# Listing experts a step behind and interleaving gate products twice a block, in a one-core decoder layer

## Chip, cores, metric

One core of a Trainium2 chip runs the whole layer in one launch. The metric is the device time in microseconds of that core. "Before" was run three times, and a further execution was profiled.

## The reference, cut to what matters

The layer has a combined projection, two groups of attention heads, an output projection, and then PEER: a retrieval of single-neuron experts by product keys. The change concerns PEER alone. T = 256 tokens, D = 2048, 16384 experts numbered 128 * ia + ib, 8 heads with 16 experts each per token:

```python
va, ia = lax.top_k(sa, PEER_TOPK)
vb, ib = lax.top_k(sb, PEER_TOPK)
...
top, sel = lax.top_k(cand, PEER_TOPK)
eidx = jnp.take_along_axis(cidx, sel, axis=-1)
gates = jax.nn.softmax(top, axis=-1)
...
act = jax.nn.gelu(jnp.einsum('thed,td->the', u[eb], xb))
w = gb * act
out = jnp.einsum('the,thed->td', w, v[eb])
```

Then come layer norms and a gated per-layer embedding.

## The kernel before, in words

PEER is done in two ways at once. The first 88 tokens are *sparse*: their rows of u and v are gathered by indirect DMA (`gb`, four buffers, 88 gathers of u and 88 of v, 1.05 MB each) and multiplied and summed on VectorE (L867, L877). The other 168 tokens (NDT) are *dense*: all of u is read and multiplied on TensorE, one block of 128 experts for each ia (L214, `ps_u`, 16 matmuls of 128x168), and GELU of it goes to a table A with a row for each expert. The rows ia 0 to 67 are part 0 (A0 and A1), ia 68 to 127 part 1 (A2). A 32-bit matmul is two instructions in the trace, so that a block of 16 matmuls is 32 of them.

`gate_work` multiplies the table by the gates. For three tokens at a time (56 groups for the 168 tokens) VectorE makes one-hot matrices of ib (`ohb`) and ia (`eq`), ScalarE scales `eq` by the two halves of the gates (`hi`, `lo`), TensorE multiplies them (`ps_G`, two matmuls per token) and counts the experts used (`ps_cnt`, one matmul per token, added up in a PSUM bank of its own over all tokens), and VectorE multiplies A by the product (L983). Each `yield` ends a step; whoever drives it decides how many steps come after a block.

`list_work` then writes A to DRAM (`s_w`), ranks the experts that any token uses, and makes lists of them: for each ia of the part, VectorE makes a one-hot row (`row`, L1069) and two columns (`blk`, L1070 and L1072), and TensorE adds their product to `ps_list` (L1074). Six such items are a step (`LISTED`). From the lists come `idxV` and `idxW`.

Part 0's gate work and list run beside the blocks ia 68 to 127 of u. Then v is done for listed experts alone, in blocks of 128: `v_fetch` gathers 128 rows of v (`vf`, five buffers shared with u's weights) and their weights (`wc`) by two indirect DMAs on GpSimd's queue, and `v_mm` adds 16 matmuls to six PSUM banks (L1199). There are 46 blocks of part 0 and 40 of part 1, fetched up to four ahead. Part 1's gate work and list run beside the first 46 blocks, four steps after each of the first 27 blocks and one after each later one; what is left is run after block 42. After block 46 a branch on a register, loaded from `total`, skips 42 spare blocks that are needed only if the lists overflow. Each engine has a branch.

`gathers(n)` paces the sparse gathers: it adds n to a sum and starts a gather for each whole one. They share GpSimd's queue with the fetches of v. The paces are GU, GUG and GUL beside blocks of u, and GVG and GV beside blocks of v. A gather waits for the buffer of the fourth before it, and the row in that buffer is used on VectorE in the order written out in the program.

`keep` holds the kept instructions of each engine in the order of the program; the matmuls of blocks and of gate products are not kept, and a scheduler places them.

Of the kernel before, what the change touches and what calls it, by code (L numbers as in the profile page):

```python
# [19 lines left out]
P = 128  # L20
# [36 lines left out]


GQ = 1.8
GU, GUG, GUL = 0.80, 0.80, 0.5  # L60
GV, GVG = 0.7, 0.65
GSCALE = 2.0 ** 15
GB = 3

LISTED = 6

EARLY, HEARLY = 5, 7
OHB = 4
# [94 lines left out]
def build(tc, a, out):  # L163
# [7 lines left out]
    def pbank(pool, name, tag="bank", bufs=4):  # L171
        return pool.tile([P, 512], F32, name=name, tag=tag, bufs=bufs)
# [765 lines left out]
            dst, dst, ALPHA, ps.rearrange("p (j t) -> p j t", j=ND)[:, :, :n],  # L938
            op0=ALU.mult, op1=ALU.add))

    def gate_work(oh, parts, s0, ns, group):


        cnt = pbank(pa, "ps_cnt")

        def one_hot(t0, n):
            def rows(x, m):
                return x[:, None, :].to_broadcast([P, n, m])

            def cols(x, m):  # L950
                return x[:, t0:t0 + n, None].to_broadcast([P, n, m])

            ohb = oh.tile([P, group, P], F16, name="ohb", tag="ohb", bufs=OHB)
            eq = oh.tile([P, group, ns], F16, name="eq", tag="eq", bufs=OHB)
            hi = oh.tile([P, group, ns], F16, name="hi", tag="hi", bufs=OHB)
            lo = oh.tile([P, group, ns], F16, name="lo", tag="lo", bufs=OHB)
            keep(nc.vector.tensor_tensor(eq[:, :n], rows(io128[:, s0:s0 + ns], ns), cols(iaT, ns),  # L957
                                         op=ALU.is_equal))
            keep(nc.vector.tensor_tensor(ohb[:, :n], rows(io128, P), cols(ibT, P),
                                         op=ALU.is_equal))  # L960
            for j in range(n):
                t = slice(t0 + j, t0 + j + 1)
                nc.scalar.mul(hi[:, j, :], eq[:, j, :], ghf[:, t])  # L963
                nc.scalar.mul(lo[:, j, :], eq[:, j, :], glf[:, t])  # L964
            return ohb, eq, hi, lo

        def product(t0, n, ohb, eq, hi, lo):
            ps = pbank(pa, "ps_G")
            for j in range(n):
                o = ps[:, j * ns:(j + 1) * ns]  # L970
                nc.tensor.matmul(o, ohb[:, j, :], hi[:, j, :], start=True, stop=False)
                nc.tensor.matmul(o, ohb[:, j, :], lo[:, j, :], start=False, stop=True)  # L972
                nc.tensor.matmul(cnt[:, :ns], ohb[:, j, :], eq[:, j, :], start=t0 + j == NSP,
                                 stop=t0 + j == T - 1)
            return ps

        def scale(t0, n, ps):
            g = ps[:, :n * ns].rearrange("p (t a) -> p a t", t=n)
            c0 = 0
            for At in parts:  # L980
                dst = At[:, :, t0 - NSP:t0 - NSP + n]
                c1 = c0 + At.shape[1]
                keep(nc.vector.scalar_tensor_tensor(dst, g[:, c0:c1], 1.0 / GSCALE, dst,  # L983
                                                    op0=ALU.mult, op1=ALU.mult))
                c0 = c1

        made, multiplied = [], None
        for t0 in list(range(NSP, T, group)) + [None] * OHB:
            if t0 is not None:
                n = min(group, T - t0)  # L990
                made.append((t0, n, one_hot(t0, n)))
            if multiplied:
                scale(*multiplied)
                multiplied = None
            yield
            if made and (len(made) > OHB - 2 or t0 is None):
                m = made.pop(0)
                multiplied = (m[0], m[1], product(m[0], m[1], *m[2]))
                yield
        if multiplied:  # L1000
            scale(*multiplied)
        yield from list_work(oh, parts, s0, ns, cnt)

    idxV, idxW, over = [], [], []

    def list_work(oh, parts, s0, ns, cnt):


        part = len(idxV)
# [7 lines left out]
        def store(n):  # L1017
            for cut in cuts[:n]:
                load(*cut)
            del cuts[:n]  # L1020

        store(2)
        m = oh.tile([P, ns], F16, name="m", tag="m")
        keep(nc.vector.tensor_scalar(m, cnt[:, :ns], 1.0, None, op0=ALU.min))
        yield
        store(1)

# [23 lines left out]
        keep(nc.vector.tensor_scalar(ov, used[:, ns:ns + 1], -float(CAPS[part] * P), 0.0,  # L1051
                                     op0=ALU.add, op1=ALU.max))
        over.append(ov)
        yield
        store(1)
        pi = oh.tile([P, SEG1], U32, name="pi", tag="pi")[:, :ns]
# [6 lines left out]
        yield  # L1063

        ps = pbank(pa, "ps_list")
        for ia in range(ns):
            row = oh.tile([P, P], F16, name="row", tag="row", bufs=2)
            blk = oh.tile([P, 2, SEG1], F16, name="blk", tag="blk", bufs=2)
            keep(nc.vector.tensor_scalar(row, io128, rank[:, ia:ia + 1], None, op0=ALU.is_equal))  # L1069
            keep(nc.vector.tensor_scalar(blk[:, 0, :ns], io128[:, :ns], pos[:, ia:ia + 1],  # L1070
                                         lin[:, 0:1], op0=ALU.is_equal, op1=ALU.mult))
            keep(nc.vector.tensor_scalar(blk[:, 1, :ns], io128[:, :ns], pos[:, ia:ia + 1],  # L1072
                                         float(ia), op0=ALU.is_equal, op1=ALU.mult))
            keep(nc.tensor.matmul(  # L1074
                ps[:, :2 * SEG1].rearrange("p (i b) -> p i b", i=2)[:, :, :ns],
                row, blk[:, :, :ns], start=ia == 0, stop=ia == ns - 1))
            if ia % LISTED == LISTED - 1:
                store(1)
                yield
        ib = oh.tile([P, SEG1 + 1], F32, name="ib", tag="used")[:, :ns]  # L1080
        iv = gin.tile([P, ns], U32, name=f"idxV{part}")
        iw = gin.tile([P, ns], U32, name=f"idxW{part}")
# [8 lines left out]
    def run(work, n):  # L1091

        for _ in range(n):
            if next(work, "end") == "end":
                return True
        return False
# [74 lines left out]
        return vf, wc  # L1171

    fetched = []
    work = gate_work(ohp, (A0, A1), *PARTS[0], GB)
    for ia in range(SEG1, NIA):
        u_block(ia, W_of(ia))

        made = ia - SEG1
        if made < 38:
            run(work, 3)  # L1180
        elif ia < NIA - 5:
            run(work, 1)
        elif ia == NIA - 5:
            while not run(work, 1):
                pass
            pools.close("a1p", "a0p")
            wcp = pools.open("wcp", "right", bufs=1)
            work = gate_work(ohp, (A2,), *PARTS[1], GB)
            run(work, 1)
        elif ia == NIA - 2:  # L1190
            run(work, 1)
        if ia >= NIA - 4:
            fetched.append(v_fetch(*order.pop(0), sup, wcp, ("wf", "wc")))
        gathers(GUG if made < 38 else GUL)
# [3 lines left out]
    def v_mm(d, vf, wc, last):  # L1198
        return nc.tensor.matmul(psv[d // 3][:, d % 3 * NDT:(d % 3 + 1) * NDT],  # L1199
                                vf[:, d * P:(d + 1) * P], wc, start=False,  # L1200
                                stop=last and (d % 3 == 2 or d == ND - 1))

    def v_bank(pool, n):

        ps = pbank(pool, "ps_v")
        keep(nc.tensor.matmul(ps[:, :n * NDT], ident, zero.to_broadcast([P, n * NDT]),
                              start=True, stop=False))
        return ps

# [5 lines left out]
            dst, dst, ALPHA, psv[b][:, :n * NDT].rearrange("p (j t) -> p j t", j=n),  # L1215
            op0=ALU.mult, op1=ALU.add))

    def v_blocks(n, wpool):

        for _ in range(n):  # L1220
            while order and len(fetched) <= LEAD and (not order[0][0] or len(idxV) > 1):
                fetched.append(v_fetch(*order.pop(0), sup, wpool, ("wf", "wc")))
            block = fetched.pop(0)
            for d in range(ND):
                v_mm(d, *block, False)

    marked = False
    psv = [v_bank(pp, 3) for _ in range(4)] + [v_bank(pa, n) for n in (3, 1)]
    done = False
    for b in range(CAPS[0]):  # L1230
        if b == CAPS[0] - LEAD:
            while not done:
                done = run(work, 1)
        v_blocks(1, wcp)
        if not done:
            done = run(work, 4 if b < 27 else 1)
        gathers(GVG if b < 27 else GV)

    fbp = pools.open("fbp", "right", bufs=1)
    total = fbp.tile([P, 1], mybir.dt.int32, name="total")  # L1240
    keep(nc.vector.tensor_tensor(total, over[0], over[1], op=ALU.add))
    more = nc.values_load(total[0:1, 0:1], min_val=0, max_val=NIA * NKEY)
    with tc.If(more > 0):
# [451 lines left out]
```

## Time and profile before

| what | us |
|---|---|
| median of 3 runs | 1829.73 |
| range of the runs | 1827.35 to 1837.43 |
| profiled execution | 1828.99 |
| its span | 1827.2 |
| busy in the span: TensorE matmuls | 1729.7 |
| VectorE | 1097.7 |
| ScalarE | 554.1 |
| GpSimd | 618.8 |

Times inside the profile count from the start of the span. PE is TensorE (PEld its weight loads), DVE VectorE, ACT ScalarE, POOL GpSimd and SP the engine that issues plain DMAs. A row of waits names the engine and its line, what it waited for, the sum, the number and the longest wait. A row of a stage gives for each engine the busy time and the instructions, then the granted TensorE clock, the DMA engines' busy share and the rate. A timeline row gives start, length, engine, line, operation and count.

### The profile page before, as it was taken

To read this page: it belongs to the slowest core of one execution; us is meant where nothing else is said; L and a number is where in the kernel's file an instruction comes from. 1 tells how busy PE (TensorE), PEld (TensorE's weight loads), DVE (VectorE), ACT (ScalarE), POOL (GpSimd) and SP (SyncE) were. 2 spreads that over 40 slices of the span, in tenths; PEclk is the share of its full clock that TensorE was granted. 3 is DMA by queue.
4 is the path that set the end of the run, shared out by engine and by line. 5 is a ranking of instruction groups with operands and counts; after the bars stand their busy time and mean duration, and the time that the engine had idled before them with its cause. 6 is when DMAs were issued, how large, how long until landed. Compare 5 with 4: busy or idle time off the path is not lost. (4 is left out here: it accounts for less than half of the span.)

```text
span 1827.2 us, 29235 instructions
## 1 busy us (share of the span) xinstructions
PE 1729.7 (95%) x11288; PEld 1594.0 (87%) x11288; DVE 1097.7 (60%) x2243; ACT 554.1 (30%) x1392; POOL 618.8 (34%) x627
## 2 busy tenths in 40 slices
PE   9999999999999999999999999799886949999998
PEld 7888888878899999999999998699886938999887
DVE  5555688654797797444577734635544372352686
ACT  5686477632111000100355410134340000000462
POOL 0233133005445227222233310344446425876000
PEclk9999999999999999999999999799898969999899
DMA  8555644756998999999999997486778929999561
GB/s 295 185 166 166 228 139 162 251 203 234 421 383 351 420 417 417 421 421 420 409 388 385 378 405 296 162 343 245 266 288 311 417 93 356 415 415 397 174 251 67
DMA packets 97105, 555.49 MB, mean 304 GB/s; under 512 B 13364, under 2 KB 16612, under 8 KB 41508
## 3 DMA queue, kind: packets, MB, share of 16 engines
q0 software_dynamic: 43152, 285.45, 39.5%
q1 hardware_dynamic: 52084, 264.99, 38.4%
q10 hardware_dynamic: 1728, 3.15, 0.5%
q8 instruction: 91, 1.49, 0.3%
q14 instruction: 50, 0.41, 0.1%
HBM read 536.67 MB, written 17.04 MB: 303 GB/s over the span
## 5 line engine op out<-in xcount | busy, mean ns | idle before, releaser
L214 PE MATMUL ps_u<-XF,wf 128*128 128x168 f32 x3936 | 594.4, 311 | 10.6 <-DMA wf<-peer_u 10.2
L214 PEld LDWEIGHTS ps_u<-XF,wf 128*128 128x128 f32 x3936 | 569.6, 192 | 21.3 <-issue 15.5
L1199 PE MATMUL ps_v<-wc,vf 128*128 128x168 f32 x2752 | 430.8, 317 | 40.1 <-DMA vf<-v_rows,idxV 24.8
L1199 PEld LDWEIGHTS ps_v<-wc,vf 128*128 128x128 f32 x2752 | 412.5, 197 | 43.9 <-issue 42.7
L124 DVE TENSOR_TENSOR wl<-wf,wh 128x1024 fp32r<-128x1024 f32 (+1 forms) x199 | 212.6, 1091 | 112.4 <-ACT wh L123 111.1
L867 DVE SCALAR_TENSOR_TENSOR gb<-gb,xq 128x2048 f32<-128x2048 f32 x88 | 202.4, 2305 | 103.6 <-DMA gb<-u_rows,eig 103.6
L123 ACT CAST wh<-wf 128x1024 fp32r<-128x1024 f32 (+1 forms) x199 | 172.1, 892 | 223.5 <-DMA wf<-ple_gate 110.6
L877 DVE SCALAR_TENSOR_TENSOR y<-gb,ew,y 128x2048 f32<-128x2048 f32 x78 | 183.0, 2346 | 84.5 <-DMA gb<-v_rows,eig 81.4
L899 POOL DMA_INDIRECT gb<-v_rows,eig x88 | 110.9, 1260 | 251.6 <-DVE eq L957 121.5
L1102 ACT ACTIVATE A<-ps_u 128x168 f32<-128x168 f32 x128 | 39.6, 310 | 488.5 <-PE ps_u L214 476.8
L202 PE MATMUL ps_qk<-X,wh 128*128 128x512 f32 x512 | 185.2, 401 | 0.0
L899 POOL DMA_INDIRECT gb<-u_rows,eig x88 | 95.1, 1081 | 258.0 <-DVE gb L867 148.3
L963 ACT ACTIVATE hi<-eq,ghf 128x68 f16<-128x68 f16 (+1 forms) x336 | 112.7, 335 | 132.3 <-DVE eq L957 110.9
L983 DVE SCALAR_TENSOR_TENSOR A<-ps_G,A 128x18 f32<-128x18 f32 (+2 forms) x168 | 46.8, 307 | 164.7 <-PE ps_G L972 133.1
L204 PE MATMUL ps_qk<-X,wl 128*128 128x256 f32 x512 | 145.7, 285 | 0.0
L1168 POOL DMA_INDIRECT vf<-v_rows,idxV x86 | 111.0, 1291 | 49.3 <-issue 20.0
L1168 POOL DMA_INDIRECT wc<-s_w,idxW x86 | 95.9, 1116 | 83.0 <-DVE ib L1086 34.2
L202 PEld LDWEIGHTS ps_qk<-X,wh 128*128 128x128 f32 x512 | 96.4, 188 | 21.9 <-issue 1.0
L214 PE MATMUL ps_q<-XF,wf 128*128 128x256 f32 x512 | 113.5, 379 | 0.0
L964 ACT ACTIVATE lo<-eq,glf 128x68 f16<-128x68 f16 (+1 forms) x336 | 112.1, 334 | 0.0
L214 PEld LDWEIGHTS ps_q<-XF,wf 128*128 128x128 f32 x512 | 95.8, 190 | 12.4
L204 PEld LDWEIGHTS ps_qk<-X,wl 128*128 128x128 f32 x512 | 96.3, 188 | 2.5 <-issue 1.3
(311 smaller groups left out, 2134.6 us busy)
## 6 DMA issues: line engine op xcount, KB each, us to landing
wf<-peer_u SPq DMA_DIRECT2D x123, 1024.0 KB
wf<-w_qk SPq DMA_DIRECT2D x64, 512.0 KB
wf<-w_out SPq DMA_DIRECT2D x32, 512.0 KB
wf<-peer_wq SPq DMA_DIRECT2D x16, 1024.0 KB
wf<-ple_gate SPq DMA_DIRECT2D x16, 1024.0 KB
s_w<-A SPq DMA_DIRECT2D x14, 672.0 KB
wf<-w_v SPq DMA_DIRECT2D x16, 512.0 KB
wf<-w_sv SPq DMA_DIRECT2D x15, 512.0 KB
```

The lines of the kernel that those rows point to most:

```text
L123: self.order(nc.scalar.copy(wh, src))
L124: self.order(nc.vector.tensor_tensor(wl, src, wh.bitcast(F32), op=ALU.subtract))
L202: nc.tensor.matmul(ps, wh[:, j * P:(j + 1) * P], xt[:, dt, :], start=dt == 0, stop=False)
L204: nc.tensor.matmul(ps[:, :T], wl[:, j * P:(j + 1) * P], xt[:, dt, :T], start=False, stop=dt == ND - 1)
L214: nc.tensor.matmul(ps[:, :T - t0], wf[:, dt * P:(dt + 1) * P], xt[:, dt, t0:], start=dt == 0, stop=dt == ND - 1)
L867: keep(nc.vector.scalar_tensor_tensor(g, g, 1.0, xq[i], op0=ALU.mult, op1=ALU.mult, accum_out=eact[i][:, j:j + 1]))
L877: keep(nc.vector.scalar_tensor_tensor(ys[i], g, ew[i][:, j:j + 1], ys[i], op0=ALU.mult, op1=ALU.add))
L899: keep(nc.gpsimd.indirect_dma_start(out=g, out_offset=None, in_=a[kind], in_offset=bass.IndirectOffsetOnAxis(ap=eig[i][:, 0, j:j + 1], axi ...
L963: nc.scalar.mul(hi[:, j, :], eq[:, j, :], ghf[:, t])
L964: nc.scalar.mul(lo[:, j, :], eq[:, j, :], glf[:, t])
L1168: keep(nc.gpsimd.indirect_dma_start(out=dst, out_offset=None, in_=src, in_offset=bass.IndirectOffsetOnAxis(ap=idx[:, b:b + 1], axis=0)))
L1199: return nc.tensor.matmul(psv[d // 3][:, d % 3 * NDT:(d % 3 + 1) * NDT], vf[:, d * P:(d + 1) * P], wc, start=False, stop=last and (d % 3 = ...
```

## The change

- The list's products are issued one step behind the items that they multiply. `row` and `blk` are taken from the buffers of the one-hot matrices, which gives twelve of each. In part 0 a step has six items as before, in part 1 three.
- Part 1's counts are no longer added up in a bank of their own. Each group's counts stand in the group's bank behind its products, and VectorE takes the first group's counts and then the maximum with each later one (`total_cnt`).
- Beside blocks of v, the steps run twice in a block, after its 8th and its 16th matmul: two steps each time until part 1's experts have been counted, then one.
- `total` is added up as soon as part 1 is counted, and its register is loaded four blocks ahead of the branch. The branch has `preferred_fallthrough_block=False`.
- Part 1's gate work starts with the first block of v: the two single steps run beside the last blocks of u are gone.
- The paces of the gathers are changed.

```diff
-GU, GUG, GUL = 0.80, 0.80, 0.5
-GV, GVG = 0.7, 0.65
+GU, GUG, GUL = 0.77, 0.80, 0.5
+GV, GVG = 0.63, 0.76
...
-LISTED = 6
...
     def product(t0, n, ohb, eq, hi, lo):
...
-                nc.tensor.matmul(cnt[:, :ns], ohb[:, j, :], eq[:, j, :], start=t0 + j == NSP,
-                                 stop=t0 + j == T - 1)
+                if counts is not None:
+                    nc.tensor.matmul(counts, ohb[:, j, :], eq[:, j, :], start=t0 + j == NSP,
+                                     stop=t0 + j == T - 1)
+            if counts is None:
+                for j in range(n):
+                    nc.tensor.matmul(ps[:, n * ns:(n + 1) * ns], ohb[:, j, :], eq[:, j, :],
+                                     start=j == 0, stop=j == n - 1)
             return ps
...
     def scale(t0, n, ps):
...
+            if counts is None:
+                new = ps[:, n * ns:(n + 1) * ns]
+                if t0 == NSP:
+                    keep(nc.vector.tensor_copy(total_cnt, new))
+                else:
+                    keep(nc.vector.tensor_tensor(total_cnt, total_cnt, new, op=ALU.max))
...
+        if part:
+            keep(nc.vector.tensor_tensor(total, over[0], over[1], op=ALU.add))
...
+        made = []
+
+        def products():
+            for ia, row, blk in made:
+                keep(nc.tensor.matmul(
+                    ps[:, :2 * SEG1].rearrange("p (i b) -> p i b", i=2)[:, :, :ns],
+                    row, blk, start=ia == 0, stop=ia == ns - 1))
+            made.clear()
+
+        new = []
         for ia in range(ns):
-            row = oh.tile([P, P], F16, name="row", tag="row", bufs=2)
-            blk = oh.tile([P, 2, SEG1], F16, name="blk", tag="blk", bufs=2)
+            if ia % 3 == 0:
+                rows = oh.tile([P, GB, P], F16, name="row", tag="ohb", bufs=OHB)
+            row = rows[:, ia % 3]
+            blk = oh.tile([P, GB, ns], F16, name="blk", tag=("eq", "hi", "lo")[ia % 3], bufs=OHB)
...
-            keep(nc.tensor.matmul(
-                ps[:, :2 * SEG1].rearrange("p (i b) -> p i b", i=2)[:, :, :ns],
-                row, blk[:, :, :ns], start=ia == 0, stop=ia == ns - 1))
-            if ia % LISTED == LISTED - 1:
+            new.append((ia, row, blk[:, :2]))
+            if ia % listed == listed - 1 or ia == ns - 1:
                 store(1)
+                products()
+                made.extend(new)
+                new = []
                 yield
+        products()
+        yield
...
-            work = gate_work(ohp, (A2,), *PARTS[1], GB)
-            run(work, 1)
-        elif ia == NIA - 2:
-            run(work, 1)
+            work = gate_work(ohp, (A2,), *PARTS[1], GB, None, 3)
...
             for d in range(ND):
                 v_mm(d, *block, False)
+                if d % 8 == 7:
+                    between()
...
+    def half():
+        nonlocal done
+        if not done:
+            done = run(work, 2 if len(over) == 1 and b < 30 else 1)
+
     for b in range(CAPS[0]):
         if b == CAPS[0] - LEAD:
             while not done:
                 done = run(work, 1)
-        v_blocks(1, wcp)
-        if not done:
-            done = run(work, 4 if b < 27 else 1)
-        gathers(GVG if b < 27 else GV)
+            more = nc.values_load(total[0:1, 0:1], min_val=0, max_val=NIA * NKEY)
+        v_blocks(1, wcp, half)
+        gathers(GVG if b < 28 else GV)
...
-    total = fbp.tile([P, 1], mybir.dt.int32, name="total")
-    keep(nc.vector.tensor_tensor(total, over[0], over[1], op=ALU.add))
-    more = nc.values_load(total[0:1, 0:1], min_val=0, max_val=NIA * NKEY)
-    with tc.If(more > 0):
+    with tc.If(more > 0, preferred_fallthrough_block=False):
```

More of the change, by code (lines that the diff above doesn't have):

```diff
@@ L939, in third_out, with gate_work @@
             op0=ALU.mult, op1=ALU.add))
-    def gate_work(oh, parts, s0, ns, group):
-        cnt = pbank(pa, "ps_cnt")
+    def gate_work(oh, parts, s0, ns, group, counts, listed):
         def one_hot(t0, n):
@@ L985, in scale @@
                 c0 = c1
+            if counts is None:
[4 more added lines that the diff above has]
+                    keep(nc.vector.tensor_tensor(total_cnt, total_cnt, new, op=ALU.max))
+        total_cnt = counts
+        if counts is None:
+            total_cnt = oh.tile([P, ns], F32, name="cnts", tag="used2")
         made, multiplied = [], None
@@ L1001, in gate_work, with list_work @@
             scale(*multiplied)
-        yield from list_work(oh, parts, s0, ns, cnt)
+        yield from list_work(oh, parts, s0, ns, total_cnt, listed)
     idxV, idxW, over = [], [], []
-    def list_work(oh, parts, s0, ns, cnt):
+    total = gin.tile([P, 1], mybir.dt.int32, name="total")
+    def list_work(oh, parts, s0, ns, cnt, listed):
         part = len(idxV)
@@ L1023, in list_work @@
         m = oh.tile([P, ns], F16, name="m", tag="m")
-        keep(nc.vector.tensor_scalar(m, cnt[:, :ns], 1.0, None, op0=ALU.min))
+        keep(nc.vector.tensor_scalar(m, cnt, 1.0, None, op0=ALU.min))
         yield
@@ L1065, in list_work @@
         ps = pbank(pa, "ps_list")
+        made = []
[6 more added lines that the diff above has]
+        new = []
         for ia in range(ns):
-            row = oh.tile([P, P], F16, name="row", tag="row", bufs=2)
-            blk = oh.tile([P, 2, SEG1], F16, name="blk", tag="blk", bufs=2)
+            if ia % 3 == 0:
+                rows = oh.tile([P, GB, P], F16, name="row", tag="ohb", bufs=OHB)
+            row = rows[:, ia % 3]
+            blk = oh.tile([P, GB, ns], F16, name="blk", tag=("eq", "hi", "lo")[ia % 3], bufs=OHB)
             keep(nc.vector.tensor_scalar(row, io128, rank[:, ia:ia + 1], None, op0=ALU.is_equal))
-            keep(nc.vector.tensor_scalar(blk[:, 0, :ns], io128[:, :ns], pos[:, ia:ia + 1],
+            keep(nc.vector.tensor_scalar(blk[:, 0], io128[:, :ns], pos[:, ia:ia + 1],
                                          lin[:, 0:1], op0=ALU.is_equal, op1=ALU.mult))
-            keep(nc.vector.tensor_scalar(blk[:, 1, :ns], io128[:, :ns], pos[:, ia:ia + 1],
+            keep(nc.vector.tensor_scalar(blk[:, 1], io128[:, :ns], pos[:, ia:ia + 1],
                                          float(ia), op0=ALU.is_equal, op1=ALU.mult))
-            keep(nc.tensor.matmul(
-                ps[:, :2 * SEG1].rearrange("p (i b) -> p i b", i=2)[:, :, :ns],
-                row, blk[:, :, :ns], start=ia == 0, stop=ia == ns - 1))
-            if ia % LISTED == LISTED - 1:
+            new.append((ia, row, blk[:, :2]))
+            if ia % listed == listed - 1 or ia == ns - 1:
                 store(1)
+                products()
+                made.extend(new)
+                new = []
                 yield
+        products()
+        yield
         ib = oh.tile([P, SEG1 + 1], F32, name="ib", tag="used")[:, :ns]
@@ L1173, in build @@
     fetched = []
-    work = gate_work(ohp, (A0, A1), *PARTS[0], GB)
+    cnt0 = pbank(pa, "ps_cnt")
+    work = gate_work(ohp, (A0, A1), *PARTS[0], GB, cnt0[:, :SEG1], 6)
     for ia in range(SEG1, NIA):
@@ L1205, in v_bank @@
         ps = pbank(pool, "ps_v")
-        keep(nc.tensor.matmul(ps[:, :n * NDT], ident, zero.to_broadcast([P, n * NDT]),
+        keep(nc.tensor.matmul(ps[:, :n], ident, zero.to_broadcast([P, n]),
                               start=True, stop=False))
@@ L1216, in v_out, with v_blocks @@
             op0=ALU.mult, op1=ALU.add))
-    def v_blocks(n, wpool):
+    def v_blocks(n, wpool, between=lambda: None):
         for _ in range(n):
@@ L1225, in v_blocks @@
                 v_mm(d, *block, False)
+                if d % 8 == 7:
+                    between()
     marked = False
-    psv = [v_bank(pp, 3) for _ in range(4)] + [v_bank(pa, n) for n in (3, 1)]
+    psv = [v_bank(pp, 3 * NDT) for _ in range(4)] + [v_bank(pa, n * NDT) for n in (3, 1)]
     done = False
+    def half():
+        nonlocal done
+        if not done:
+            done = run(work, 2 if len(over) == 1 and b < 30 else 1)
     for b in range(CAPS[0]):
```

## The prediction

> **What bounds the kernel now.** I read the page's head first, then TensorE's waits, then its busy time cut into the stages the change touches, then single timeline rows for prices.
>
> ```profile
> span 1827.2 us, 29235 instructions
> PE 1729.7 (95%) x11288; PEld 1594.0 (87%) x11288; DVE 1097.7 (60%) x2243; ACT 554.1 (30%) x1392; POOL 618.8 (34%) x627
> ```
> TensorE is busy for 95% of the span, so only its idle time and its slow time can be won. Its waits over the whole span:
>
> ```profile
> PE ps_v L1199 <- DMA vf<-v_rows,idxV: 24.8, 9, 5.2
> PE ps_list L1074 <- DVE blk L1072: 23.7, 68, 2.5
> PE ps_v L1199 <- PEq L1243: 14.7, 1, 14.7
> ```
> All three lie where the change works. By stage (time, busy by engine, granted clock, DMA share and GB/s):
>
> ```profile
> core 0: us, PE busy (x) PEld busy (x) DVE busy (x) ACT busy (x) POOL busy (x), PEclk, DMA share, GB/s
> 1088.50:1190.60 102.10, 83.50 (x518) 76.03 (x516) 56.08 (x217) 10.20 (x38) 20.24 (x23) 0.85 0.64 249
> 1199.70:1280.00 80.30, 80.30 (x737) 78.94 (x734) 44.17 (x81) 35.59 (x144) 38.11 (x33) 1.00 0.74 275
> 1280.00:1380.00 100.00, 84.13 (x723) 81.56 (x719) 53.04 (x97) 41.19 (x168) 45.30 (x38) 0.91 0.70 261
> 1380.00:1438.70 58.70, 44.36 (x272) 43.17 (x273) 20.38 (x28) 0.00 (x0) 36.35 (x30) 0.85 0.96 385
> 1438.70:1506.90 68.20, 43.40 (x287) 37.16 (x284) 47.23 (x186) 0.00 (x0) 20.04 (x18) 0.80 0.51 199
> 1506.90:1540.00 33.10, 29.38 (x183) 29.15 (x184) 6.77 (x4) 0.00 (x0) 18.06 (x17) 0.90 0.86 336
> 1540.00:1620.00 80.00, 79.40 (x562) 79.31 (x561) 30.66 (x16) 4.43 (x8) 62.61 (x51) 1.00 1.02 414
> ```
> The rows are: list of part 0 beside blocks of u; gate products of part 1 beside blocks of v (two rows); the stores of part 1's weights; its list and the branch; the blocks after it; a stage that runs well. The second and the last show TensorE full at clock 1.00; in the others it idles and the clock falls too, so their loss is more than the idle time. The block matmuls alone, for v and then for u:
>
> ```profile
> 1199.70:1280.00 80.30, 78.61 (x503) 71.75 (x501) 1.00 0.74 275
> 1280.00:1380.00 100.00, 78.51 (x460) 72.95 (x460) 0.91 0.70 261
> 1380.00:1438.70 58.70, 43.53 (x256) 42.32 (x256) 0.85 0.96 385
> 1438.70:1506.90 68.20, 34.55 (x227) 32.27 (x225) 0.80 0.51 199
> 1506.90:1540.00 33.10, 29.38 (x183) 29.15 (x184) 0.90 0.86 336
> ```
> ```profile
> 1088.50:1190.60 102.10, 74.60 (x450) 70.69 (x448) 0.85 0.64 249
> ```
> Their price at full speed, from start to start of neighbouring rows:
>
> ```profile
> 1074.74 13.92 PE L214 MATMUL ps_u<-XF,wf 128*128 128x168 f32 x96
> 1088.49 0.28 PE L1074 MATMUL ps_list<-blk,row 128*128 128x136 f16 x2
> ...
> 1455.50 0.22 PE L1074 MATMUL ps_list<-blk,row 128*128 128x120 f16 x1
> 1455.55 2.79 PE L1199 MATMUL ps_v<-wc,vf 128*128 128x168 f32 x18
> ...
> 1575.78 45.77 PE L1199 MATMUL ps_v<-wc,vf 128*128 128x168 f32 x320
> 1621.27 0.51 PE L920 MATMUL ps_yn<-wh,sel 128*64 128x512 f32 x1
> ```
> 320 matmuls in 45.49 us are 0.142 each, so a block of v (32) takes 4.55 us; for u it is 13.75/96 = 0.143; a list product takes 0.05 of TensorE when its operands are there. In 1199.7 to 1280 the other 234 matmuls are 26 groups of 9 gate products: (80.3 - 503 x 0.142)/26 = 0.34 each.
>
> So the floors, and what each stage loses over them: part 0's list 450 x 0.143 + 68 x 0.05 = 67.8, loss 34.3. Gate stage from 1280: 460 x 0.142 + 29 x 0.34 = 75.2, loss 24.8. Stores: 256 x 0.142 + 1 = 37.4, loss 21.3. List and branch: 227 x 0.142 + 60 x 0.05 = 35.2, loss 33.0. After the branch: 183 x 0.142 = 26.0, loss 7.1. Together 120.5 us.
>
> **Part by part. List products.** Before, row and blk have two buffers, so each product waits for three VectorE operations made just ahead of it. In the instruction order 28 products of part 0, and 36 of part 1, stand in a row with no block between them: TensorE goes at VectorE's pace. The change has twelve buffers and issues a step's products one step later. In its order part 0 has nine sets of six, each a block of u (16 matmul pairs) apart, then 14 nearly together; part 1's stand in threes, half a block apart, from block 32.1 to 41.0, so the list ends five blocks ahead of the branch. VectorE's pace and what remains:
>
> ```profile
> 1490.71 0.25 DVE L1069 TENSOR_SCALAR row<-io,rank 128x128 f16<-128x128 f16 x1
> 1490.88 0.30 DVE L1070 TENSOR_SCALAR blk<-io,pos,lin 128x60 f16<-128x60 f16 x1
> 1491.08 0.23 DVE L1072 TENSOR_SCALAR blk<-io,pos 128x60 f16<-128x60 f16 x1
> 1491.23 0.25 DVE L1069 TENSOR_SCALAR row<-io,rank 128x128 f16<-128x128 f16 x1
> ```
> ```profile
> PE ps_u L214 <- DMA wf<-peer_u: 4.5, 3, 1.9
> ```
> 0.52 us an item. Six per block of u are 3.1 of 4.9 us; six per block of v, with 0.63 gathers of 2.35 us (row below), 4.6 of 4.9: it fits, barely. For part 0 I leave the 4.5 us of waits for u's weights (the second row is from 1040 to 1200), 4 for the last 14 products (7.3 of VectorE, 12 pairs of 0.29 beside them) and 2 of slow clock: gain 34.3 - 10.5 = 24. Bounds: 34 (all gone), 12 (28 items' 14.6 us and the weights' waits stay, with their slow clock).
>
> **Gate products.** The number of matmuls is the same (three per token). The counts move into the group's own bank and are added by a maximum on VectorE, 56 times. Part 1 keeps no bank for counts, so groups have two banks instead of one. The instruction order shows the main thing: before, the 21st group stands after 13.9 blocks of v and the last after 31.6; now the 21st stands after 11.0 and the last after 28.5, one each half block. Before, VectorE held up its gathers' sums behind late groups, GpSimd's queue held a gather for their buffers, and the fetch of vf behind it came late:
>
> ```profile
> POOL gb L899 <- DVE eq L957: 72.2, 9, 11.3
> DVE y L877 <- DMA gb<-v_rows,eig: 38.7, 8, 12.6
> ...
> L877 DVE SCALAR_TENSOR_TENSOR y<-gb,ew,y 128x2048 f32<-128x2048 f32 x37 | 86.9, 2348 | 41.8 <-DMA gb<-v_rows,eig 38.7 <-issue 3.0
> L1168 POOL DMA_INDIRECT vf<-v_rows,idxV x55 | 66.4, 1207 | 35.9 <-issue 12.4 <-PE ps_cnt L973 6.3 <-PE ps_v L1199 6.2
> L959 DVE TENSOR_TENSOR ohb<-io,ibT 128x384 f16<-128x384 f16 x52 | 28.6, 550 | 0.0
> L983 DVE SCALAR_TENSOR_TENSOR A<-ps_G,A 128x180 f32<-128x180 f32 x56 | 20.9, 373 | 107.2 <-PE ps_G L972 80.3 <-PE ps_cnt L973 20.8 <-PE ps_v L1199 5.7
> L957 DVE TENSOR_TENSOR eq<-io,iaT 128x180 f16<-128x180 f16 x52 | 17.5, 336 | 0.0
> L1047 DVE TENSOR_TENSOR rank<-used,pos 128x60 f32<-128x60 f32 x1 | 0.2, 221 | 0.0
> ```
> The maximum is not in this trace; its nearest row is 221 ns (bounds 0 and 0.37, the scale's). At most a group then costs VectorE 0.55 + 0.37 + 0.34 + 0.22 = 1.48, two per block 3.0, and 0.76 gathers 1.8: 4.8 of the 5.2 us of a block. It fits, so it hides; without that cover each group would add up to 0.22 us, 12 in all. I leave 4 us of single waits: gain 21 (bounds 25 and 0).
>
> **Stores, list 1, branch.** From 1380 to 1540 the DMA moved 385 x 58.7 + 199 x 68.2 + 336 x 33.1 = 47.3 MB in 160 us, half-idle beside the list. At the 414 GB/s of the good stage this is 114 us; 1.4 gathers less (0.63 for 0.70 over 20 blocks) make it 111. TensorE's floor is 37.4 + 35.2 + 26.0 = 98.6, and the branch adds:
>
> ```profile
> L1243 PEldq COMPARE_BRANCH x1: 5681/5681/5681, 1500.9 to 1500.9; - x1
> ```
> 5.7 us beyond the wait for `total`, which is now added blocks earlier and loaded ahead. On SP, ScalarE and VectorE the load waits for a sum long made; on GpSimd it stands just ahead of part 1's first fetch, which needs the list, made later. The eight stores (5.2 MB, 12.5 us of DMA) still leave at once; four blocks fetched ahead (18 us) cover most. I take 117 between the floor 104 and 123 (47.3 MB at the 385 of the stores' stage): gain 43.
>
> The changed order still jumps over the 42 spare blocks on TensorE, so I keep the 5.7; without, 1737. [...]
>
> **The paces.** Two gathers move from u's stage to v's; at the end three gathers stand together with five blocks (23 us) left for three sums more: I take 2 us (0 to 6).
>
> Sum: 24 + 21 + 43 - 2 = 86 us. The profiled execution took 1828.99 us, 1.8 outside its span and 0.7 below the median of three, 1829.73. Forecast 1743 us, with its own range from 1720 to 1766.
>
> [...]
>
> **Rivals.** *The copies set the pace* (0.20): 123 us from 1380 to 1540, half of the gate stage's loss stays since fetches still queue behind gathers, and part 0 waits 6 us more for weights: 37 + 12 + 18 - 2 = 65, 1764 us. For it: DMA shares of 0.96 and 1.02. Against: TensorE ran full at 1.02.
> *VectorE sets the pace* (0.08): a late gather holds its queue (12.6 us at worst above) and every group or item behind it, and TensorE, which now meets them each half block, stops as often. The gate stage gains nothing and list 0 half: 12 + 0 + 30 - 2 = 40, 1789 us. Against: the 4.8 of 5.2 us above, worked out with every bound at its worse end.
> *GpSimd's queue* (0.05, slower): each of the 0.76 gathers per block holds it for h us. With 1.25 us per issue a block takes 0.76 (h + 1.25) + 2.5 against 5.2; it decides from h = 2.3. At the mean hold above (72.2/9 = 8.0) that is 9.5 us, 4.3 more for 28 blocks, 120: 1863 us. It cancels the whole gain at h = 6.4, where a block takes 3.1 us more. Against: two banks and a regular order let VectorE keep up.
> *It does nothing* (0.02): the waits only change their names, 1829.
>
> **Numbers.** Forecast 0.65, rivals 0.20, 0.08, 0.05, 0.02. All but the last two lie over 0.5% (9 us, about what a measurement of this kernel tells from none) below 1829.73: faster 0.92, slower 0.05, same 0.03. The range goes from 1716 (all losses gone but the branch: 1714) to 1785, in which the first two cases lie.
>
> **What would show it.** Right: TensorE's wait of ps_list for blk under 6 us in total, of ps_v for vf under 12, the branch wait near 6; a clock near 1.00 from 1200 on; v blocks without the half-idle DMA row of 0.51. Wrong: GpSimd's hold at gb for VectorE still near 70 us, or TensorE waiting for VectorE in each half block.

## The result

| what | before | after |
|---|---|---|
| median, us | 1828.54 | 1733.79 |
| range of the runs | 1827.12 to 1837.43 | 1730.71 to 1734.96 |
| profiled execution | 1828.99 | 1734.96 |

The ratio is 0.9467, with a 95% interval from 0.9439 to 0.9496. The forecast was 1743, its own range 1720 to 1766. In the profiles the span went from 1827.2 to 1733.2, by 94.0 us; the forecast's sum was 86.

The head of the page of the changed kernel:

```profile
span 1733.2 us, 29306 instructions
PE 1696.1 (98%) x11288; PEld 1574.4 (91%) x11288; DVE 1100.7 (64%) x2299; ACT 553.9 (32%) x1392; POOL 607.2 (35%) x625
```

TensorE's waits over the whole span, those for operands of the blocks:

```profile
PE ps_v L1228 <- DMA vf<-v_rows,idxV: 15.3, 3, 6.6
PE ps_u L212 <- DMA wf<-peer_u: 6.0, 22, 1.1
```

The wait of `ps_list` for `blk` (23.7 before) is gone, that for `vf` has fallen from 9 to 3, and no wait for `ps_cnt` is left. The three that remain are one at the branch (6.6 us) and two at the very end (8.7 together). To see where the time came from, both traces are cut at the same matmuls of v, of which each has 2752 recorded (86 blocks of 32). The cuts of the prediction at 1280, 1380 and 1540 us stand behind 533, 992 and 1655 of them, that is at block 16.7, 31.0 and 51.7. After, the stretches from the first v matmul on are:

```profile
core 0: us, PE busy (x) PEld busy (x) DVE busy (x) ACT busy (x) POOL busy (x), PEclk, DMA share, GB/s
1160.70:1251.90 91.20, 91.20 (x836) 87.42 (x835) 62.43 (x139) 46.21 (x187) 49.54 (x51) 1.00 0.99 391
1251.90:1326.20 74.30, 74.30 (x681) 72.70 (x680) 52.88 (x110) 30.99 (x126) 41.26 (x39) 1.00 0.98 374
1326.20:1433.90 107.70, 101.09 (x726) 99.62 (x725) 66.92 (x205) 0.00 (x0) 67.58 (x58) 0.97 0.95 384
1433.90:1575.80 141.90, 141.90 (x996) 141.32 (x995) 52.30 (x36) 4.43 (x8) 100.47 (x79) 1.00 0.98 391
1575.80:1623.60 47.80, 37.49 (x218) 35.93 (x217) 16.85 (x28) 7.38 (x15) 5.22 (x3) 0.75 0.42 161
```

The same blocks before (the row from 1280 is in the prediction):

```profile
1190.60:1280.00 89.40, 89.40 (x781) 85.67 (x779) 44.17 (x81) 35.90 (x145) 40.93 (x36) 1.00 0.77 290
1380.00:1540.00 160.00, 117.13 (x739) 109.48 (x740) 74.39 (x217) 0.00 (x0) 74.46 (x64) 0.84 0.75 295
1540.00:1682.80 142.80, 142.20 (x997) 141.53 (x996) 58.58 (x38) 4.43 (x8) 108.80 (x86) 1.00 1.01 413
1682.80:1717.80 35.00, 33.27 (x218) 32.63 (x217) 13.14 (x26) 7.38 (x15) 0.00 (x0) 0.85 0.47 161
```

| stretch | before | after | gained | forecast |
|---|---|---|---|---|
| up to the first v matmul | 1190.6 | 1160.7 | 29.9 | 24 |
| blocks of v to 16.7 | 89.4 | 91.2 | -1.8 | 0 |
| to 31.0 (gate products) | 100.0 | 74.3 | 25.7 | 21 |
| to 51.7 (stores, list 1, branch) | 160.0 | 107.7 | 52.3 | 43 |
| to 82.1 | 142.8 | 141.9 | 0.9 | 0 |
| to 86 (the end of v, paces) | 35.0 | 47.8 | -12.8 | -2 |
| behind v | 109.4 | 109.6 | -0.2 | 0 |

Two things stand out. From the first v matmul to block 82 the idle time is gone but for 6.6 us: in the rows of after, PE is as long as the stretch, except in the third row, where 107.70 - 101.09 is the wait at the branch. And the last four blocks, which nothing in the change touches but the paces, take 12.8 us more.

### The profile page after: what moved, and what is told of

Read it like the earlier page. It is cut to its first block, busy times and chain, and to the rows that moved or that the text cites. A ratio compares the mean times of both kernels' runs of the same rounds, so it can differ in the third digit from the quotient of the medians.

```text
span 1733.2 us, 29306 instructions
## 1 busy us (share of the span) xinstructions
PE 1696.1 (98%) x11288; PEld 1574.4 (91%) x11288; DVE 1100.7 (64%) x2299; ACT 553.9 (32%) x1392; POOL 607.2 (35%) x625
## 4 chain that ended last, share of the span: by engine, by line
PE 80%; DMA 13%; DVE 3%; issue 2%; POOL 2%; ACT 1%; POOLq 0%; ACTq 0%; SPq 0%; DVEq 0%
PE ps_u L212 27%; PE ps_v L1228 17%; DMA wf<-peer_u 8%; PE ps_qk L200 7%; PE ps_q L212 6%; PE ps_qk L202 4%; PE ps_v L219 2%; PE ps_v L221 2%; PE ps_v L220 2%; PE ps_gate L219 1%; PE ps_gate L221 1%; PE ps_gate L220 1%; PE ps_mix L220 1%; PE ps_mix L221 1%; PE ps_mix L219 1%
## 5 line engine op out<-in xcount | busy, mean ns | idle before, releaser
L212 PE MATMUL ps_u<-XF,wf 128*128 128x168 f32 x3936 | 584.0, 308 | 6.8 <-DMA wf<-peer_u 6.0
L212 PEld LDWEIGHTS ps_u<-XF,wf 128*128 128x128 f32 x3936 | 562.6, 190 | 14.1 <-issue 8.8
L1228 PE MATMUL ps_v<-wc,vf 128*128 128x168 f32 x2752 | 420.8, 311 | 15.3 <-DMA vf<-v_rows,idxV 15.3
L1228 PEld LDWEIGHTS ps_v<-wc,vf 128*128 128x128 f32 x2752 | 399.9, 192 | 18.0 <-issue 16.8
L897 POOL DMA_INDIRECT gb<-v_rows,eig x88 | 102.5, 1164 | 125.2 <-DVE eq L956 34.7
```

Of the source, the lines that this page charges most:

```text
L212: nc.tensor.matmul(ps[:, :T - t0], wf[:, dt * P:(dt + 1) * P], xt[:, dt, t0:], start=dt == 0, stop=dt == ND - 1)
L897: keep(nc.gpsimd.indirect_dma_start(out=g, out_offset=None, in_=a[kind], in_offset=bass.IndirectOffsetOnAxis(ap=eig[i][:, 0, j:j + 1], axi ...
```

## The experiments

My theory: the lists held TensorE at VectorE's pace; late gate groups held VectorE, behind it GpSimd's queue, and so the fetches of v; the end's loss is from three gathers issued together. The rivals: the gain is the paces'; it is the half-block steps', not the bank's; it is the branch's flag's or its early load's. Each run was compared with runs of the kernel before on the same chip; ratios are to those. The medians of the kernel before lie between 1828.5 and 1831.8 us in these comparisons, so that a few us between two experiments tell nothing.

**The list's change alone** (before, with the list's part of the diff shown earlier, six items a step in both parts).

> The kernel before with the list's change alone: a step's products go out one step later, with twelve buffers, six items a step in both parts; gate products, counts, branch and paces as before. Theory A (the lists cost TensorE because it ran at VectorE's pace): part 0's wait of ps_list for blk goes and its stage loses the 29.9 us by which the changed kernel's first v matmul came earlier (1190.6 to 1160.7), so the first v matmul comes near 1162. Part 1's list still begins at block 40 instead of 32, since its gate groups lag as before, and only part of the 33 us of its stage is won: some 10 to 15. Time 1783 to 1795. Rival B (the list's gain came from fewer gathers beside u, by the paces): the first v matmul stays within 8 us of 1190.6, time above 1810. The gate stage keeps its GpSimd holds at gb near 72 us by both.

1789.28 us, ratio 0.9759 [0.9736, 0.9783]. In its trace the first v matmul, and TensorE's waits between 1040 and 1195:

```profile
1170.38 2.71 PE L1221 MATMUL ps_v<-zero,ident 128*128 128x504 f32 x6
```
```profile
PE ps_u L214 <- DMA wf<-peer_u: 7.9, 4, 4.0
```

And its stretches from block 16.7 to 31.0 and on to 51.7, then GpSimd's wait between 1160 and 1420:

```profile
1260.00:1358.60 98.60, 81.26 (x718) 78.60 (x717) 52.81 (x97) 41.11 (x168) 44.17 (x37) 0.95 0.70 264
1358.60:1500.60 142.00, 111.22 (x740) 107.99 (x741) 74.08 (x218) 0.00 (x0) 79.09 (x63) 0.88 0.84 329
```
```profile
POOL gb L899 <- DVE eq L957: 71.7, 11, 10.7
```

The total is as theory A had it, and B falls: the list alone brings 20.3 us at the first v matmul (1190.6 to 1170.4) and 18.0 in part 1 (160 to 142.0), over the 10 to 15 expected, and leaves the gate stage nearly as it was (98.6 for 100.0, GpSimd's hold 71.7 for 72.2). Part 0 misses the expected 1162 by 8 us: all waits for `blk` are gone, but waits for u's weights, 4.5 us before, are 7.9 now. The stage of part 0's list shows this without the differences that stand ahead of it. From the same matmul of u (448 before the end of u) to the first v matmul, before, with the list alone, and in the changed kernel:

```profile
1090.10:1190.60 100.50, 83.22 (x514) 75.92 (x515) 54.95 (x211) 9.89 (x37) 20.24 (x23) 0.85 0.64 246
1093.60:1170.30 76.70, 70.82 (x516) 69.72 (x517) 46.77 (x186) 9.78 (x37) 20.28 (x23) 0.98 0.82 328
1090.80:1160.70 69.90, 68.98 (x516) 68.02 (x517) 49.35 (x188) 9.67 (x37) 19.46 (x19) 1.00 0.79 316
```

The list alone takes 23.8 us out of the stage, and the whole change 30.6; the 6.8 between them are about what the waits for u's weights fell by, from 7.9 us there to 0.9 in the changed kernel.

**The paces alone** (before, with the paces of after).

```diff
-GU, GUG, GUL = 0.80, 0.80, 0.5
-GV, GVG = 0.7, 0.65
+GU, GUG, GUL = 0.77, 0.80, 0.5
+GV, GVG = 0.63, 0.76
...
-        gathers(GVG if b < 27 else GV)
+        gathers(GVG if b < 28 else GV)
```

> The kernel before with the changed kernel's paces alone. Theory A (lists, late groups and the branch make the gain; the paces only move gathers out of u's stage): 0 to 10 us faster than 1830, since the first v matmul, which the list alone brought to 1170.4 and the whole change to 1160.7, comes up to 9.7 us earlier, but more gathers (0.76 for 0.65 a block) meet late groups and three gathers stand together at the end. Rival B (the paces made much of the gain): 30 us or more.

1835.09 us, ratio 1.0007 [0.9990, 1.0024]: no change. The first v matmul stays at 1190.4, against my expectation: while the list sets the pace, fewer gathers beside u buy nothing. Its last four blocks take 46.6 us (1678.2 to 1724.8) for 35.0, so the loss at the end comes with the paces alone. Rival B is out.

**The old paces** in the changed kernel (the reverse of that diff).

> The changed kernel with the paces of before. Theory A: the first v matmul comes 5 to 10 us later (near 1168) because u's stage has its two gathers back, and the end, without three gathers together, wins some 8 to 10 back: 1728 to 1736. Rival B (the paces made much of the gain): 1750 or more. Rival C (the 9.7 us of u's stage are from the two single gate steps that are gone, not from the gathers): the first v matmul stays within 3 us of 1161 and the time is 1722 to 1727.

1730.76 us, ratio 0.9440 [0.9418, 0.9462]. The first v matmul comes at 1165.4 and the last four blocks take 35.1 us for 47.8. A holds in total, B falls, and the time of C (1722 to 1727) didn't come. How much of the 4.7 us at the first v matmul is the paces' stays open: in eight kernels that are the same up to there (after and seven below) it lies between 1154.6 and 1162.1, and their waits for u's weights in the list's stage are 0.9 to 2.5 us. Here they are 5.2 us, but they are 5.6 in a kernel below that has the new paces (the list's products in the same step).

**The counts on TensorE again**, so one bank fewer for gate groups.

```diff
-            work = gate_work(ohp, (A2,), *PARTS[1], GB, None, 3)
+            cnt1 = pbank(pa, "ps_cnt")
+            work = gate_work(ohp, (A2,), *PARTS[1], GB, cnt1[:, :SEG2], 3)
```

> The changed kernel with part 1's counts added up in a TensorE bank of their own again, so one bank fewer for the gate groups, and no maximum on VectorE; steps still twice a block. In the instruction order the groups then stand 0.62 to 0.69 of a block apart, not 0.50, the last after 32.0 blocks and not 28.5, and list 1's products begin at 34.8 and not 32.1. Theory A (the second bank lets groups keep their place, and late groups held VectorE, GpSimd's queue and the fetches): GpSimd's hold at gb for VectorE comes back towards 72 us, v's wait for vf to some 20 us, the clock between 1250 and 1380 falls to 0.9, and 15 to 25 us of the gain go: 1750 to 1760. Rival B (twice a block does it, the bank is nothing): within 4 us of 1734.

1762.47 us, ratio 0.9614 [0.9594, 0.9635], 28.7 us over the changed kernel. GpSimd's wait between 1160 and 1420 and, of TensorE, that over the whole span:

```profile
POOL gb L897 <- DVE eq L956: 57.5, 12, 9.3
```
```profile
PE ps_v L1229 <- DMA vf<-v_rows,idxV: 23.5, 10, 6.5
```

The chain can be read on GpSimd's timeline (at the end of a row, the idle time before and what ended it):

```profile
1296.25 1.04 POOL L1199 DMA_INDIRECT vf<-v_rows,idxV  x1 [0.30 <-PE ps_cnt L973]
1304.53 1.26 POOL L897 DMA_INDIRECT gb<-v_rows,eig  x1 [7.24 <-DVE eq L956]
1306.09 0.95 POOL L1199 DMA_INDIRECT wc<-s_w,idxW  x1 [0.30 <-issue]
1307.35 0.94 POOL L1199 DMA_INDIRECT vf<-v_rows,idxV  x1 [0.30 <-issue]
```

and its two stretches:

```profile
1248.90:1337.30 88.40, 78.18 (x722) 75.94 (x720) 56.39 (x96) 41.47 (x170) 47.09 (x42) 0.98 0.86 316
1337.30:1463.20 125.90, 108.82 (x739) 104.93 (x740) 72.49 (x217) 0.00 (x0) 74.45 (x65) 0.95 0.94 374
```

A gather stands 7.24 us for VectorE, and the fetch of the next block leaves behind it, 11 us after the last. In the changed kernel GpSimd has no wait for `eq` in that stretch. So the bank is worth 14.1 us in the gate stage (88.4 for 74.3) and 18.2 behind it (125.9 for 107.7), where TensorE waits 6.7 us for `vf` and 5.2 for the list's items. That this second part comes from the later start of the list is argued from the order of the program. A holds in its mechanism, but its price was too low: 28.7 us went, not 15 to 25, and the clock was expected at 0.9 in the gate stage and is 0.98.

**Steps once a block** (two banks and VectorE's counts stay).

```diff
-                if d % 8 == 7:
+                if d == ND - 1:
...
-            done = run(work, 2 if len(over) == 1 and b < 30 else 1)
+            done = run(work, 4 if len(over) == 1 and b < 30 else 2)
```

> The changed kernel with its steps once a block (four, then two), not twice; two banks and VectorE's counts stay. In the instruction order two groups then stand together at each block's end (1.0, 2.0, 2.0, 3.0, 3.1 ... 29.0), on average where they stood before the edit. Theory A (it is the lag of the groups that cost, and the bank that took it away): VectorE's four operations per group come in bunches of two but none is late, so the time stays within 6 us of 1734. Rival B (twice a block makes the gain of the gate stage): most of its 21 us go, 1750 or more, with TensorE waiting for VectorE or ScalarE at the second of each two groups.

1732.41 us, ratio 0.9457 [0.9441, 0.9473], the same as the changed kernel. A holds, B falls: with two banks, twice a block buys nothing.

**The list's products in the same step.**

```diff
             if ia % listed == listed - 1 or ia == ns - 1:
                 store(1)
-                products()
                 made.extend(new)
                 new = []
+                products()
                 yield
```

> The changed kernel with a step's list products issued in the same step as the items they multiply; the twelve buffers stay. In part 1's order that moves the products only half a block ahead (the last at 40.5, not 41.0). Theory A (the buffers, with a block of matmuls between the sets, carry it; a whole step's lag is more than is needed): TensorE meets each set of six some 3 us too early at most in part 0, and waits of ps_list for blk come back to a part of the 23.7 us of before: 5 to 15 us, time 1740 to 1750. Rival B (a step's lag is what matters, twelve buffers alone are nothing): the whole 24 us of part 0's list come back, 1755 to 1760. Rival C (buffers alone): within 3 us of 1734 with no such wait.

1736.33 us, ratio 0.9481 [0.9461, 0.9501], inside the changed kernel's interval. Of the waits of `ps_list` only 0.5 us come back: with the twelve buffers the step behind is not needed (rival C). No run has the step behind with two buffers.

**The branch's flag, and its load.** One kernel leaves out `preferred_fallthrough_block=False`; the other loads the register just ahead of the branch:

```diff
-            more = nc.values_load(total[0:1, 0:1], min_val=0, max_val=NIA * NKEY)
         v_blocks(1, wcp, half)
         gathers(GVG if b < 28 else GV)
...
+    more = nc.values_load(total[0:1, 0:1], min_val=0, max_val=NIA * NKEY)
     with tc.If(more > 0, preferred_fallthrough_block=False):
```

> The changed kernel without preferred_fallthrough_block=False. Theory A (in the changed order TensorE jumps over the spare blocks either way, and the 6.2 us of the branch do not depend on which block follows): within 3 us of 1734, the branch again 5.5 to 6.5 us. Rival B (the flag saved something): 5 us or more slower. Rival C: faster by the 6 us, if without the flag nothing is jumped over.

> The changed kernel with the branch's register loaded just ahead of the branch, as before; the sum it loads is still made blocks earlier. Theory A (before, TensorE waited 14.7 us at the branch because the list and its sum came last; the load itself is little): 0 to 3 us slower than 1734. Rival B (the load ahead is what took the wait from 14.7 to 6.6): TensorE waits 10 to 15 us there again and the time is 1738 to 1744.

1732.88 us, ratio 0.9464 [0.9444, 0.9484], and 1734.72, 0.9469 [0.9452, 0.9487]: both the same as the changed kernel. TensorE's instructions at the branch (count, nanoseconds least/median/most, first and last start), of after, without the flag, and the load in the third:

```profile
L1276 PEldq COMPARE_BRANCH  x2: 95/3136/6177, 1397.5 to 1399.8; - x2
```
```profile
L1276 PEldq COMPARE_BRANCH  x1: 6146/6146/6146, 1401.3 to 1401.3; - x1
```
```profile
L1275 PEldq TENSOR_LOAD <-total x1: 486/486/486, 1401.2 to 1401.2; - x1
```

With the flag there are two branches, and the second costs what the one cost; the load is 0.5 us. Theory A holds for both times, and neither flag nor load took the wait from 14.7 to 6.6 us. On TensorE, though, the second of these runs moved little: in the changed kernel too its load starts only at 1396.9, 0.6 us ahead of its branches. What moved is the sum: VectorE adds up `total` at 1500.1 before, with TensorE already waiting, and at 1323.9 in the changed kernel. No run puts the sum alone back behind the list, so that its share is argued from these times.

**No branch** (the 42 spare blocks are left out with it).

> The changed kernel without the branch: the 42 spare blocks behind it are left out, so this gives the price of the branch alone. Theory A: TensorE's wait of 6.6 us at the branch goes, and GpSimd's 11 us, in which it waits there for its own DMAs, so that the fetches and gathers behind are earlier too: 6 to 12 us faster than the changed kernel, 1722 to 1728. Rival B: the blocks behind wait for their fetches anyway (the DMA moves 243 GB/s there): under 3 us.

1723.59 us, ratio 0.9413 [0.9392, 0.9435]: 10.2 us by the medians. Blocks 44 to 50, in after and here:

```profile
1390.20:1426.10 35.90, 29.30 (x195) 29.07 (x195) 8.34 (x4) 0.00 (x0) 18.75 (x16) 0.90 0.81 316
```
```profile
1386.00:1413.10 27.10, 27.10 (x193) 27.10 (x192) 8.34 (x4) 0.00 (x0) 20.93 (x18) 1.00 1.01 415
```

8.8 us are lost right there: 6.6 idle, and the rest at a mean clock of 0.90. A holds.

**The end's gathers: GV 0.67, and 0.70**, for 0.63.

```diff
-GV, GVG = 0.63, 0.76
+GV, GVG = 0.67, 0.76
```

> The changed kernel with GV 0.67 in place of 0.63, so that the gathers left over at the end do not stand three together. Theory A (three gathers together made the last three fetches late and left TensorE waiting 6, 5.3 and 3.3 us and at half clock, some 12 us): the last blocks run without waits, 1722 to 1730. Rival B (that much data just has to be moved: the same gathers, only earlier, delay fetches elsewhere): within 4 us of 1734.

> The changed kernel with GV 0.70 alone (0.67 gave 1724, 0.63 gives 1734). Theory A (what counts is that no three gathers stand together ahead of the last fetches): like 0.67, 1721 to 1728. Rival B (each gather less in these stages is time won): 5 us slower than 0.67, 1729 or more, since the DMA's share is already 1.02 there.

1724.27 us, ratio 0.9412 [0.9395, 0.9429], and 1726.87, 0.9424 [0.9400, 0.9448]. First the end of the changed kernel, GpSimd's timeline and TensorE's:

```profile
1559.79 2.49 POOL L897 DMA_INDIRECT gb<-v_rows,eig  x1 [0.48 <-DMA wc<-s_w,idxW]
1562.59 0.94 POOL L897 DMA_INDIRECT gb<-v_rows,eig  x1 [0.30 <-issue]
1569.68 0.94 POOL L897 DMA_INDIRECT gb<-v_rows,eig  x1 [6.16 <-DVE gb L875]
1570.92 0.95 POOL L1199 DMA_INDIRECT wc<-s_w,idxW  x1 [0.30 <-issue]
1572.17 0.94 POOL L1199 DMA_INDIRECT vf<-v_rows,idxV  x1 [0.30 <-issue]
```
```profile
1569.83 10.94 PE L1228 MATMUL ps_v<-wc,vf 128*128 128x168 f32 x74
1586.10 0.90 PE L1228 MATMUL ps_v<-wc,vf 128*128 128x168 f32 x2 [5.33 <-DMA vf<-v_rows,idxV]
1590.34 3.82 PE L1228 MATMUL ps_v<-wc,vf 128*128 128x168 f32 x14 [3.34 <-DMA vf<-v_rows,idxV]
```

Three gathers in a row need three buffers; the third stands 6.16 us for VectorE to use one, and the last three fetches behind it leave from 1572.2 on, for blocks that TensorE reaches from 1581. It waits 5.33 and 3.34 us, and the clock is 0.75 over the stretch: 18 matmuls of v from 1604.8 on take 5.39 us, the 18 from 1611.2 on 2.73. With 0.67 the last four blocks are

```profile
1581.00:1614.70 33.70, 31.85 (x219) 31.34 (x219) 13.14 (x26) 7.38 (x15) 0.00 (x0) 0.90 0.48 164
```

33.7 us for 47.8, and no wait for `vf` is left. A holds for both: at neither pace do three gathers stand together there, and the higher pace brings nothing more. No run keeps 0.63 and spreads the three, so that the pace and their standing together are not told apart.

**Both: GV 0.67 and steps once a block.**

> The changed kernel with GV 0.67 and steps once a block: is it the best? Theory A (twice a block is worth nothing, the pace 10 us): within 3 us of 1724. Rival B (the two meet: bunches of two groups hold gathers when these are more): 1728 or more.

1724.31 us, ratio 0.9405 [0.9385, 0.9426]: as good as 0.67 alone, which is the simpler edit. These two are the best versions found that keep the branch, some 9.5 us under the changed kernel.

## Why the prediction was right

The direction and the main mechanisms held, and the time came out 9 us lower. Four terms were mis-sized, three to one side and one to the other, so that the nearness of the total is in part luck: 21 us of gain that I had not counted stand against 13 of loss.

- **List of part 0**, 24 forecast, 29.9 gained. The waits for `blk` all went. I left 10.5 us over the floor of the stage: 4.5 for waits on u's weights, 4 for the last 14 products and 2 of slow clock. With the list alone 8.9 are left (76.7 for 67.8), 7.9 of them those waits, so that its 23.8 us are the forecast's 24 with other terms inside. In the changed kernel 2.1 are left: eleven of the last products go in one row of 0.82 us, and the waits are 0.9. What took these away, paces, the missing single steps or chance, the runs don't decide.
- **Gate products**, 21 forecast, 25.7 gained, just beyond my bound of 25. The 4 us "of single waits" didn't come: PE is 74.30 of 74.30 us. And groups moved, which I had not priced: those that no longer lag fall into the stretch before, so that 681 matmuls stand here for 723, and 836 there for 781. That is six groups more, 2.0 us at 0.34 each, and that stretch took 1.8 us longer, where I had put nothing. The lag's chain, groups, VectorE, GpSimd's queue, fetch, is shown by the run with the counts on TensorE. I gave the half-block steps a part in it; with two banks they have none. What else makes up the other 12 us, between 100.0 and the 88.4 of that run, was not taken apart.
- **The maximum** was bounded by 0 and 0.37 us and taken as 0.22; it took 0.207, and hid. **VectorE** was busy for 52.88 of 74.30 us in that stage: its rival (0.08) didn't come. Nor did GpSimd's (0.05), which decides from a hold of 2.3 us for each gather: between 1160 and 1420 GpSimd stood for VectorE at `gb` for 12.5 us in all, over 36 gathers, 0.35 us each.
- **Stores, list 1 and branch**, 117 us forecast, 107.7 measured: 101.1 of TensorE's own work and 6.6 us at the branch. I let the copies have a say between the floor and 123, and carried over some 46 MB. Only 41.4 MB were left here (384 GB/s x 107.7 us), since more went out in the blocks ahead: 35.7 MB up to block 16.7 (391 x 91.2), 25.9 before (290 x 89.4). But for the 6.6 us at the branch TensorE waited for no copy here, so the rival in which they set the pace (0.20) falls too. That the branch would keep its 5.7 us was right: 6.2 in the row, and the flag changes nothing. Its full price is higher than the 6 us that I put on it, 8.8 where it stands. Why it lasts so long no run shows: on TensorE it took 4.27 us with the list alone, 5.68 before, and 5.96 to 6.18 in the changed kernel and the two runs on its flag and load. Without the 5.7 the sum was 1737.
- **The end** is the step that failed: 2 us (bounds 0 and 6), and 12.8 measured. I saw the three gathers together and priced the sums that VectorE had still to make, 23 us of blocks for three. The cost was elsewhere: the third gather holds GpSimd's queue for a buffer (6.16 us), and the last fetches of v stand behind it. It is the mechanism that the prediction used for the gate stage and for its slower rival, and I did not apply it here.
- **The clock.** Before, TensorE idled for 15.9 us in the gate stage, no wait there was longer than 2.5 us, and the clock was 0.91. I counted the slow clock with the idle time, 24.8 us; with the idle time alone the forecast would have been 8.9 us higher, 1752. The stage gained 25.7, 1.7 of them by the five groups that left it (0.34 each), so the 24.8 with the slow clock is nearer. How the clock goes with idle time the runs don't show: with the counts on TensorE the stretch idles for 10.2 of 88.4 us at a clock of 0.98, before for 15.9 of 100 at 0.91.

Of the signs that I named, the list's wait under 6 us and the branch near 6 came, the clock up to block 82, and no row of half-idle DMA before that. `vf` reads 15.3, over the 12, but 6.6 of it is the wait at the branch, which the view puts down to `vf`; the other two waits, 8.7 us, are the end's.

## What to carry to other kernels

When a queue issues transfers of several kinds, ask of each instruction in it which buffer it waits for and which fetch stands behind it, at the ends of loops too, where a paced flow is emptied at once: here the last three gathers went with a loss of 12.8 us beside a gain of 94. Running the steps twice a block instead of once bought nothing; one bank more let each group keep its place, and that was worth 28.7 us. Price a loop's consumer and its operands' buffers before moving the products in time: with twelve buffers the step behind brought nothing that these runs can tell.

## What was not expected of the hardware

With GV 0.67 the clock falls without a wait. I had read it as following waits. TensorE has no gap from 1574.7 to 1601 there, but between two stretches of v stand 64 recorded matmuls of 32 columns:

```profile
1592.71 0.39 PE L929 MATMUL ps_y<-sel,gb 128*128 128x32 f32 x2
1592.93 0.52 PE L929 MATMUL ps_y<-sel,y 128*128 128x32 f32 x2
1593.26 0.61 PE L929 MATMUL ps_y<-sel,gb 128*128 128x32 f32 x2
...
1597.10 4.16 PE L1228 MATMUL ps_v<-wc,vf 128*128 128x168 f32 x18
...
1605.75 2.73 PE L1228 MATMUL ps_v<-wc,vf 128*128 128x168 f32 x18
```

From 1593 on a pair starts every 0.43 us, not every 0.22, some 5 us after the first of them at 1588.1. The next 18 matmuls of v take 4.16 us, not 2.73, and the granted clock is 0.90 over the last four blocks (1581.0 to 1614.7). That these slow rows are the fall is read from the changed kernel, where pairs start every 0.43 us from 1597.1 on, behind its two waits, and the granted clock is 0.50 from there to 1604.8. Why it falls was not tried.

At the branch GpSimd loses more than TensorE: in the changed kernel its next fetch leaves 11.36 us after the last instruction, behind four semaphore events and an instruction of 1402 ns on its queue.

```profile
L1276 POOLq EVENT_SEMAPHORE  x4: 17/43/43, 1403.0 to 1408.1; - x4
L1276 POOLq INC_SWDGE_SEM  x1: 1402/1402/1402, 1408.2 to 1408.2; - x1
```
```profile
1410.87 0.95 POOL L1199 DMA_INDIRECT wc<-s_w,idxW  x1 [11.36 <-issue]
```

In the same gap the view names the gather of `gb` before (10.37 us) and without the flag (12.1 us), and in the changed kernel VectorE's wait for a gather ends at 1408.11, as the last of the four events starts (1408.1). That this is a wait for GpSimd's own transfers is argued from these times and was not tried.
